# Differential attention scores from full-precision, unsplit queries and keys, a head's two maps as two 64-row products

## The chip, the cores and the metric

The kernel runs on one NeuronCore of a Trainium2 chip. The metric is the device time of one execution in microseconds (us); a lower time is better. Five engines matter here: TensorE (PE in the profile; its weight loads are a row of their own, PEld), VectorE (DVE), ScalarE (ACT), GpSimd (POOL) and SyncE (SP), which issues nearly all DMA transfers. TensorE reads its operands from SBUF, a memory of 128 partitions, and writes to PSUM, which has eight banks of 512 fp32 values in each partition.

## What is computed

The reference is one encoder layer, applied to two groups (prompt and sample) of 1024 tokens with 1024 channels. One projection of the normalised input yields the queries, keys and values of two attention branches and several gates. Branch A is grouped-query attention with 8 heads of 64 dimensions. Branch B is the part that the change touches:

```python
qb = rms_norm(qb.reshape(B, S, H_B, 2, HEAD_DIM), qn_b)      # 4 heads, 2 maps, 64 dims
kb = rms_norm(kb.reshape(B, S, H_B, 2, HEAD_DIM), kn_b)
...                                                           # partial rotary on q and k
s = jnp.einsum('bqhmd,bkhmd->bhmqk', qblk, k) * scale
p = jax.nn.softmax(s, axis=-1)
pd = p[:, :, 0] - lam * p[:, :, 1]
return jnp.einsum('bhqk,bkhe->bqhe', pd, v)                   # 128-dim values
```

Each head of B thus has two score maps of 1024 x 1024. The sum over d in a score has 64 terms. Afterwards both branches are gated, projected, merged and projected once more.

## The kernel before, in words

**Split operands.** Nearly all products run in a TensorE data type (float32r) that takes one pass but keeps fewer bits than fp32. To regain precision, an operand x is split into a high part (a copy rounded to float32r) and a low part (x minus the high part), and the products high-high, high-low and low-high are added in PSUM. `proj_tt` (L497) and `z_gen` (L679) do so with three matmuls for each chunk of the input projection.

**Queries and keys of B.** `qkb_gen` projects the queries and keys of one head, 128 tokens at a time (8 token tiles, `tt`). `rms` and `rope` normalise and rotate them, mostly on POOL. `pairs_T` then transposes them on TensorE (L548) into a PSUM bank, in which partitions 0 to 63 hold map 0 and 64 to 127 hold map 1. For each map it writes one tile that holds the high part in 64 partitions and the low part in the other 64: two ACT copies (L550, 64 x 256) and two DVE subtractions (L551, 64 x 256) for each token tile. A head keeps two such tiles of 128 x 2048 (from `utile`, a pool of 15), one for each map, and each holds queries and keys.

**Scores.** Since high and low parts are stacked in the 128 rows, one matmul gives high-high plus low-low. The crosswise terms need the same queries with the halves exchanged: `swapped` makes that copy with DMAs (L574), two for each map and pair of query tiles. `softmax_unit` computes one map for 128 queries and 1024 keys: for each half of the keys a matmul with the queries (L709) and one with the swapped queries (L710), into a score tile of two PSUM banks (`sbank`; the pool `ps_s` has two of them, so both are in use when two maps are under way). DVE takes the row maximum (L711), and ACT the exponential with its sum (L712), which frees the score tile. `scores` calls this once for each map. After map 1 it also computes the factor lambda x sum0 / sum1 (L731 on DVE, L732 on POOL). `flip` combines the two maps (L744), transposes in blocks (L745), and sends the result through four DMAs (L750). `b_values` multiplies it with the values (L810). The values of B are kept unsplit in fp32 already, so L810 is a full-precision product; the trace shows each as two weight loads and two matmul instructions.

**Order of the work.** `attention` writes the attention as a list of small steps. A unit is 256 queries of one head. In B a unit has four score steps (query tile 0 map 0, map 1, query tile 1 map 0, map 1) and seven value steps that start 1.4 units later. `weave` interleaves these steps with the projections (`qkb_gen`, `vb_gen`, `z_gen`) by shares of progress: `phase` counts `4 * (9 + PV_LAG)`, that is 44, attention steps for a head of B, and the stretch with the last head counts `LAST_ATT`, 48. Attention steps are given a priority 100 instructions ahead of their place (`AHEAD`). A scheduler then fixes the order of the instructions on each engine before the run, by priority among those it takes to be ready. On the chip every engine keeps that order and waits on semaphores.

**Counts.** Two groups, four heads and eight query tiles make 64 query tiles of B, each with two maps. The B score products number 2 x 2 x 128 = 512: 256 on L709 and 256 on L710. Scores of B (L709 writing s from a tile u) start at 512 us for the first group and near 1460 us for the second. Branch A's scores run on the same lines with another operand pair (s from u and u).

Of the kernel before, what the change touches and what calls it, by code (L numbers as in the profile page):

```python
# [12 lines left out]
F32 = mybir.dt.float32  # L13
# [77 lines left out]
def kernel(ctx: ExitStack, tc: tile.TileContext, t: dict):  # L91
# [23 lines left out]
    def sbank():  # L115
        return ps_s.tile([P, 1024], F32, tag="s", name=nm("s"))
# [13 lines left out]
    def utile():  # L130
        return upool.tile([P, 2048], F32R, tag="u", name=nm("u"))
# [448 lines left out]
    def v2(u):  # L580
        return u.rearrange("p (h n) -> p h n", h=2)
# [43 lines left out]

    def qkb_gen(ht, out, h):
        w = load_w(w_cols(w_in, (C_QB + h * P, P), (C_KB + h * P, P)))
        qk = out[h] = (v2(utile()), v2(utile()))

        def front(tt, ps):  # L630
            e = by_turns(tt)
            x3, s3 = rms(ps, 4, e)
            x4 = x3.rearrange("p (a m) d -> p a m d", a=2)
            e.tensor_tensor(out=x4, in0=x4, in1=gB.unsqueeze(2).to_broadcast([P, 2, 2, HD]), op=ALU.mult)
            rope(x3[:, :, :16], s3[:, :, :16], cosB[:, tt], sinB[:, tt], 8, e)
            return x3

        def back(tt, x3):
            sl = slice(tt * P, (tt + 1) * P)
            pairs_T(x3, qk[0][:, :, sl], qk[1][:, :, sl])  # L640
            made[id(qk)] = tt + 1

        yield from pipelined(ht, w, front, back)
# [56 lines left out]
    def piece_order(x):  # L700
        return x.rearrange("p (i t b) -> p i t b", t=2, i=4)

    def softmax_unit(q, sw, k, pt, su):

        m = tiny.tile([P, 1], F32, tag="m", name=nm("m"))
        s = sbank()
        for n in range(2):
            sl = slice(n * 512, (n + 1) * 512)
            nc.tensor.matmul(s[:, sl], q, k[:, sl], start=True, stop=False)  # L709
            nc.tensor.matmul(s[:, sl], sw, k[:, sl], start=False, stop=True)  # L710
        nc.vector.tensor_reduce(out=m, in_=s, axis=AX.X, op=ALU.max, negate=True)  # L711
        nc.scalar.activation(  # L712
            pt.rearrange("p (j c a) -> p j c a", j=4, c=8), s.rearrange("p (c a j) -> p j c a", c=8, j=4),
            AF.Exp, bias=m, accum_out=su,
        )

    def scores(u, i):

        nm_ = len(u["q"])
        t, m = i // nm_, i % nm_  # L720
        qt = u["pr"] * 2 + t
        if "sw" not in u:
            u["sw"] = swapped(u)
        pt = ptile()
        su = u["su"][:, qt : qt + 1] if m == 0 else tiny.tile([P, 1], F32, tag="su", name=nm("su"))
        softmax_unit(u["q"][m][:, qt * P : (qt + 1) * P], u["sw"][:, m, t * P : (t + 1) * P], u["k"][m], pt, su)
        if m == 0:
            u[t] = [pt]
        else:
            f = tiny.tile([P, 1], F32, tag="r", name=nm("r"))  # L730
            nc.vector.reciprocal(f, su)  # L731
            nc.gpsimd.tensor_scalar(  # L732
                out=f, in0=f, scalar1=u["su"][:, qt : qt + 1], scalar2=nlam, op0=ALU.mult, op1=ALU.mult
            )
            u[t] += [pt, f]
        return t if m == nm_ - 1 else None

    def flip(u, t):

# [103 lines left out]
    def attention(units):  # L843


        steps = []
        for n, (ph, _, _) in enumerate(units):
            na, nv = (2, 4 + PV_LAG) if ph < 2 else (4, 5 + PV_LAG)
            steps += [(n + i / na, ph, n, i, True) for i in range(na)]
            steps += [(n + BEHIND + i / nv, ph, n, i, False) for i in range(nv)]  # L850
        steps.sort(key=lambda x: x[0])
        live, vals, late = {}, {}, []
        last = max(x[1] for x in steps)
        cur = 0
        for at, ph, n, i, qk in steps:
            if qk:
                while cur < ph:
                    cur += 1
                    yield cur
            with tc.high_priority(offset=AHEAD):  # L860
                if qk:
                    if n not in live:
                        live[n] = units[n][1]()
                    t = scores(live[n], i)
                else:
                    t = None
                    if n not in vals:
                        vals[n] = (a_values if ph < 2 else b_values)(live[n])
                    next(vals[n], None)
                for todo in late:  # L870
                    todo()
                late = []
                if t is not None:
                    late.append(lambda u=live[n], t=t: flip(u, t))
                    if t == (0 if ph < 2 else 0) and n + 1 < len(units) and units[n + 1][2]():
                        live[n + 1] = units[n + 1][1]()
                        late.append(lambda u=live[n + 1]: u.update(sw=swapped(u)))
            yield None
        for todo in late:
            todo()  # L880
# [135 lines left out]
    def units_of(st):  # L1016

        def a_unit(half, i, pr):
            j = half * 4 + i
            kv = j // 4  # L1020
            return {
                "q": [st["qa"][half][i % 2][:, i // 2]], "k": [st["ka"][:, kv]],
                "v": (lambda k: st["va"][:, k, kv, :]),
                "pr": pr, "j": j, "od": st["od"][j // 2], "su": st["suA"][:, j],
            }

        def b_unit(h, pr):
            qk = st["qkb"][h]
            return {
                "q": [qk[m][:, 0] for m in range(2)], "k": [qk[m][:, 1] for m in range(2)],  # L1030
                "v": st["vb"][h], "pr": pr, "h": h,
                "od": st["od"][4 + h], "ss": st["ssB"], "su": st["suB"][:, h],
            }

        def there(kind, n, pr):
            return made.get(id(st[kind].get(n)), 0) > 2 * pr + 1

        units = []
        for half in range(2):
            units += [  # L1040
                (half, lambda a=(half, i, pr): a_unit(*a), lambda a=("qa", half, pr): there(*a))
                for i in (0, 2, 1, 3) for pr in range(4)
            ]
        for h in range(4):
            units += [
                (2 + h, lambda a=(h, pr): b_unit(*a), lambda a=("qkb", h, pr): there(*a)) for pr in range(4)
            ]
        return units
# [23 lines left out]
    for g in range(2):  # L1072
        st = states[g]
        ht = st["ht"]
        load_tables_A(st)
        zs = chain(*[z_item(st, i) for i in range(12)])
        head(g, st, zs, late)
        alone[0] = False
        if g == 0:
            load_tables_B()  # L1080

        att = attention(units_of(st))

        def phase(k, *fs, more=()):
            n_att = 16 * (6 + PV_LAG) if k < 2 else 4 * (9 + PV_LAG)
            nz = 3 * Z_SHARE[g][k]
            weave(
                (until_next(att), n_att * ATT_W[g][k], 0.0), (chain(*fs), 31 * len(fs), IN_A[g][k]),
                (islice(zs, nz), nz, Z_A[g][k]), *more,
            )  # L1090

        phase(0, qa_gen(st, 1))
        phase(1, vb_gen(ht, st["vb"], 0), qkb_gen(ht, st["qkb"], 0))
        oT, mT = ([], []), ([], [])
        for h in range(4):
            fs = []
            if h < 3:
                fs.append(qkb_gen(ht, st["qkb"], h + 1))
            if h == 1:
                fs.append(vb_gen(ht, st["vb"], 1))  # L1100
            if h < 3:
                phase(2 + h, *fs)

        first = chain(*[gated_gen(st, i, hf, oT[hf]) for i in range(2) for hf in range(2)])
        then = [[gated_gen(st, i, hf, oT[hf]) for hf in range(2)] for i in (2, 3)]

        def gates():
            yield from first
            yield from chain(*then[0])

        def fill():
            if g == 0:
                yield from gate_gen()
            yield from zs
            drain(first)
            yield from islice(merge, 16 - TAIL)

        merge = merge_gen(st, 0, oT, mT)

        weave((until_next(att), LAST_ATT, 0.0), (fill(), LAST_FILL, 0.0), (gates(), 12, GATED_A))  # L1120
        alone[0] = True
        weave((merge, TAIL, 0.0), (then[1][0], 2, TAIL_A))
        weave((merge_gen(st, 1, oT, mT), 8, 0.0), (then[1][1], 4, 1.0))
        if g == 0:
            weave((out_gen(g, mT), 16, 0.0), (ht_gen(1, states[1]["ht"]), 13, -0.1))
        else:
            drain(out_gen(g, mT))
# [54 lines left out]
```

## Time and profile before

| | |
|---|---|
| median of 3 runs | 1982.26 us (1980.13 to 1987.66) |
| span of the profiled execution | 1985.5 us (the profile gives no other time for it) |
| TensorE busy with matmuls / weight loads | 1908.6 us (96%) / 1627.8 us (82%) |
| DVE / ACT / POOL busy | 1330.8 (67%) / 1009.9 (51%) / 758.1 us (38%) |
| mean granted TensorE clock | 0.982 |
| DMA | 295.11 MB |

The span runs from the first to the last instruction of one execution; it stands 3.2 us above the median of the runs. Busy times are unions of the instructions' records. A matmul's record is longer than its share of the array, since consecutive matmuls overlap at their ends, so the cost of a matmul is read from the distance of starts in a long row of equal ones. In the tables of instruction groups a row reads: line, engine, operation, output from inputs, shape, count, then busy time and mean ns of one, then idle time of the engine ahead of it and what ended that.

### The profile page before, as it was taken

The numbers are of one execution on the slowest core, as the hardware profiler recorded it, in microseconds if no ns is written. First come the engines' busy times: TensorE is split into PE (matmuls) and PEld (weight loads), VectorE is DVE, ScalarE is ACT, GpSimd is POOL, SyncE is SP. The second block draws the span as 40 slices with busy tenths as digits, with TensorE's granted clock in tenths as the row PEclk, the third lists the DMA queues.
The fourth block names the chain that finished last, engine by engine and source line by source line (L and its number), as shares of the span: only waits on it lengthen the run. The fifth ranks groups of instructions, "written<-read, shape, count | busy, mean of one in ns | idle before, by whom it ended". The sixth has DMA issues, their size and how long they took to land.

```text
span 1985.5 us, 30670 instructions
## 1 busy us (share of the span) xinstructions
PE 1908.6 (96%) x10466; PEld 1627.8 (82%) x10466; DVE 1330.8 (67%) x1906; ACT 1009.9 (51%) x1939; POOL 758.1 (38%) x1008
## 2 busy tenths in 40 slices
PE   8889999999999998999999899999999999999999
PEld 3878888888878994778888787888887888877887
DVE  4558877777877577547465877677788845665641
ACT  4435655665654444754323565556655534566310
POOL 2374612453446252221235464134445626422110
PEclk9899999999999999999999999999999999999999
DMA  8124556555553345865641455565654333567532
GB/s 310 33 80 126 155 152 169 152 166 154 133 153 102 101 120 173 257 227 167 222 149 35 140 144 145 149 164 144 184 137 137 106 97 99 156 212 245 174 101 75
DMA packets 269531, 295.11 MB, mean 149 GB/s; under 512 B 35776, under 2 KB 218176, under 8 KB 269376
## 3 DMA queue, kind: packets, MB, share of 16 engines
q1 hardware_dynamic: 269376, 293.15, 49.7%
q8 instruction: 84, 1.38, 0.3%
q14 instruction: 71, 0.58, 0.1%
HBM read 133.59 MB, written 42.01 MB: 88 GB/s over the span
## 4 chain that ended last, share of the span: by engine, by line
PE 68%; DMA 8%; DVE 8%; ACT 5%; SPq 4%; issue 3%; POOL 3%; ACTq 0%; POOLq 0%; DVEq 0%
PE f L497 16%; PE f L679 16%; PE f L950 6%; PE f L979 5%; PE s L709 4%; PE a L810 4%; PE s L710 4%; PE s L979 4%; DMA q<-p 3%; SPq L750 3%; PE s L950 2%; DVE q L759 2%; PE a L771 2%; PE a L770 2%; DVE m L711 2%
## 5 line engine op out<-in xcount | busy, mean ns | idle before, releaser
L679 PE MATMUL f<-u,w 128*128 128x512 f32 x2232 | 582.3, 398 | 0.1
L497 PE MATMUL f<-w,u 128*128 128x256 f32 x3456 | 487.0, 286 | 2.2 <-ACT ev L685 1.4
L497 PEld LDWEIGHTS f<-w,u 128*128 128x128 f32 x3456 | 459.5, 192 | 22.4 <-ACT ev L685 1.8
L679 PEld LDWEIGHTS f<-u,w 128*128 128x128 f32 x2232 | 408.8, 190 | 77.3 <-POOL w L181 0.8
L181 POOL TENSOR_TENSOR w<-st,w 128x512 fp32r<-128x512 f32 x168 | 230.3, 1390 | 439.9 <-ACT w L179 375.1
L712 ACT ACTIVATE p<-s,m 128x1024 f32<-128x1024 f32 x256 | 284.4, 1111 | 206.3 <-DVE m L711 111.3
L711 DVE TENSOR_REDUCE m<-s 128x1 f32<-128x1024 f32 x256 | 310.0, 1216 | 51.3 <-PE s L710 48.7
L745 DVE STREAM_TRANSPOSE p<-p 128x1024 f32<-128x1024 f32 x192 | 238.2, 1241 | 99.2 <-ACT p L712 86.5
L759 DVE TENSOR_TENSOR q<-q,hi 128x512 fp32r<-128x512 f32 x256 | 198.3, 792 | 60.6 <-ACT hi L758 58.6
L515 POOL TENSOR_TENSOR rs<-ss,nhalf 128x4 f32<-128x4 f32 (+1 forms) x112 | 112.8, 1007 | 322.8 <-DVE ss L514 284.0
L758 ACT ACTIVATE hi<-q 128x512 fp32r<-128x512 f32 x256 | 153.8, 625 | 104.1 <-DMA q<-p 55.4
L710 PE MATMUL s<-u,sw 128*128 128x512 f32 x512 | 206.7, 404 | 0.0
L179 ACT ACTIVATE w<-st 128x512 fp32r<-128x512 f32 x196 | 113.9, 625 | 97.2 <-DMA st<-in_w_in_dram 46.0
L950 PE MATMUL f<-u,w 128*128 128x512 f32 x552 | 133.4, 395 | 5.1 <-ACT ev L685 4.4
L770 PE MATMUL a<-hi,u 128*128 128x256 f32 x512 | 132.5, 285 | 2.1 <-DVE oo L787 2.1
L771 PE MATMUL a<-q,u 128*128 128x256 f32 x512 | 129.8, 286 | 1.2 <-DVE q L759 1.2
L810 PE MATMUL a<-q,u 128*128 128x256 f32 x512 | 128.3, 390 | 1.9 <-DVE oo L826 1.5
L950 PEld LDWEIGHTS f<-u,w 128*128 128x128 f32 x552 | 103.9, 190 | 27.2 <-ACT ev L685 4.7
L709 PE MATMUL s<-u 128*128 128x512 f32 x256 | 110.9, 433 | 15.1 <-ACT p L712 15.1
L810 PEld LDWEIGHTS a<-q,u 128*128 128x128 f32 x512 | 97.8, 196 | 17.5 <-DVE oo L826 1.6
L709 PE MATMUL s<-u,u 128*128 128x512 f32 x256 | 103.6, 405 | 8.3 <-ACT p L712 7.7
L710 PEld LDWEIGHTS s<-u,sw 128*128 128x128 f32 x512 | 98.4, 192 | 15.5
(175 smaller groups left out, 2562.1 us busy)
## 6 DMA issues: line engine op xcount, KB each, us to landing
q<-p SPq DMA_DIRECT2D x768, 128.0 KB, 2.6
st<-in_w_in_dram SPq DMA_DIRECT2D x132, 256.0 KB, 3.0
zd<-ev SPq DMA_DIRECT2D x96, 256.0 KB, 2.2
sw<-u SPq DMA_DIRECT2D x256, 64.0 KB, 2.1
p<-zd SPq DMA_DIRECT2D x64, 256.0 KB, 3.2
u<-in_w_ada_dram SPq DMA_DIRECT2D x8, 1024.0 KB, 10.4
st<-in_w_in_dram SPq DMA_DIRECT2D x64, 128.0 KB, 2.7
st<-in_w_out_dram SPq DMA_DIRECT2D x32, 256.0 KB, 2.9
```

The costliest lines, as they stand in the source:

```text
L181: e.tensor_tensor(out=wl, in0=st, in1=wh.bitcast(F32), op=ALU.subtract)
L497: nc.tensor.matmul(ps, lt[c][:, sl], w[:, c, wi, :], start=(k == 0), stop=(k == 23))
L679: nc.tensor.matmul(ps, w[:, c, wi, e * P : (e + 1) * P], rt[c], start=(k == 0), stop=(k == 23),)
L709: nc.tensor.matmul(s[:, sl], q, k[:, sl], start=True, stop=False)
L710: nc.tensor.matmul(s[:, sl], sw, k[:, sl], start=False, stop=True)
L711: nc.vector.tensor_reduce(out=m, in_=s, axis=AX.X, op=ALU.max, negate=True)
L712: nc.scalar.activation(pt.rearrange("p (j c a) -> p j c a", j=4, c=8), s.rearrange("p (c a j) -> p j c a", c=8, j=4), AF.Exp, bias=m, accu ...
L745: nc.vector.transpose(pt, pt)
L759: nc.vector.tensor_tensor(out=tl, in0=tl.bitcast(F32), in1=th.bitcast(F32), op=ALU.subtract)
L810: nc.tensor.matmul(acc, u["v"][:, k], pT[:, k], start=(k == 0), stop=(k == 7))
L950: nc.tensor.matmul(ps, w[:, c, wi, d * P : (d + 1) * P], o[:, oi, :], start=(k == 0), stop=(k == 11))
L979: nc.tensor.matmul(ps, w[:, c, wi, e * P : (e + 1) * P], m[:, mi, :], start=(k == 0), stop=(k == 23))
```

## The change

The queries and keys of B are no longer split. Each head has one fp32 tile of 128 x 2048: map 0 in partitions 0 to 63, map 1 in 64 to 127, queries in the first half of the columns and keys in the second. `qkb_gen` fills it with one ACT copy of 128 x 256 for each token tile. `scores_b` computes both maps of a query tile in one step: for each half of the keys one fp32 product for map 0 (64 rows, into the first score tile) and one for map 1 (the other 64 rows, into the second). Maximum, exponential and factor follow as before. The swapped copies are not made for B. A unit of B has two score steps in place of four, and `phase` counts 36 steps for a head; `LAST_ATT` stays 48. Branch A does what it did.

```diff
     def qkb_gen(ht, out, h):
         w = load_w(w_cols(w_in, (C_QB + h * P, P), (C_KB + h * P, P)))
-        qk = out[h] = (v2(utile()), v2(utile()))
+        qk = out[h] = v2(utile().bitcast(F32))
...
         def back(tt, x3):
-            sl = slice(tt * P, (tt + 1) * P)
-            pairs_T(x3, qk[0][:, :, sl], qk[1][:, :, sl])
+            ps = gbank()[:, : 2 * P].rearrange("p (b n) -> p b n", b=2)
+            x = x3.rearrange("p (b two) d -> p b (two d)", two=2)
+            for b in range(2):
+                nc.tensor.transpose(ps[:, b, :], x[:, b, :], ident)
+            nc.scalar.activation(qk[:, :, tt * P : (tt + 1) * P], ps, AF.Copy)
             made[id(qk)] = tt + 1
...
+    def scores_b(u, t):
+        qt = u["pr"] * 2 + t
+        ss = [sbank(), sbank()]
+        for n in range(2):
+            sl = slice(n * 512, (n + 1) * 512)
+            for s, rows in zip(ss, (LO, HI)):
+                nc.tensor.matmul(
+                    s[:, sl], u["qk"][rows, 0, qt * P : (qt + 1) * P], u["qk"][rows, 1, sl], start=True, stop=True
+                )
+        pts = [ptile(), ptile()]
+        sus = [u["su"][:, qt : qt + 1], tiny.tile([P, 1], F32, tag="su", name=nm("su"))]
+        for s, pt, su in zip(ss, pts, sus):
+            softmax(s, pt, su)
+        f = tiny.tile([P, 1], F32, tag="r", name=nm("r"))
+        nc.vector.reciprocal(f, sus[1])
+        nc.gpsimd.tensor_scalar(out=f, in0=f, scalar1=sus[0], scalar2=nlam, op0=ALU.mult, op1=ALU.mult)
+        u[t] = [*pts, f]
+        return t
...
-            na, nv = (2, 4 + PV_LAG) if ph < 2 else (4, 5 + PV_LAG)
+            na, nv = (2, 4 + PV_LAG) if ph < 2 else (2, 5 + PV_LAG)
...
-                        late.append(lambda u=live[n + 1]: u.update(sw=swapped(u)))
+                        if ph < 2 and "q" in live[n + 1]:
+                            late.append(lambda u=live[n + 1]: u.update(sw=swapped(u)))
...
-            n_att = 16 * (6 + PV_LAG) if k < 2 else 4 * (9 + PV_LAG)
+            n_att = 16 * (6 + PV_LAG) if k < 2 else 4 * (7 + PV_LAG)
```

`softmax` is the second half of `softmax_unit` (maximum and exponential), taken out as a function; `LO` and `HI` are the partition slices 0 to 63 and 64 to 127.

More of the change, by code (lines that the diff above doesn't have):

```diff
@@ L701, in piece_order, with softmax @@
         return x.rearrange("p (i t b) -> p i t b", t=2, i=4)
+    def softmax(s, pt, su):
+        m = tiny.tile([P, 1], F32, tag="m", name=nm("m"))
+        nc.vector.tensor_reduce(out=m, in_=s, axis=AX.X, op=ALU.max, negate=True)
+        nc.scalar.activation(
+            pt.rearrange("p (j c a) -> p j c a", j=4, c=8), s.rearrange("p (c a j) -> p j c a", c=8, j=4),
+            AF.Exp, bias=m, accum_out=su,
+        )
     def softmax_unit(q, sw, k, pt, su):
-        m = tiny.tile([P, 1], F32, tag="m", name=nm("m"))
         s = sbank()
@@ L710, in softmax_unit @@
             nc.tensor.matmul(s[:, sl], sw, k[:, sl], start=False, stop=True)
[L711 to L715, printed above, removed]
+        softmax(s, pt, su)
[7 more added lines that the diff above has]
+                    s[:, sl], u["qk"][rows, 0, qt * P : (qt + 1) * P], u["qk"][rows, 1, sl], start=True, stop=True
+                )
+        pts = [ptile(), ptile()]
+        sus = [u["su"][:, qt : qt + 1], tiny.tile([P, 1], F32, tag="su", name=nm("su"))]
+        for s, pt, su in zip(ss, pts, sus):
+            softmax(s, pt, su)
+        f = tiny.tile([P, 1], F32, tag="r", name=nm("r"))
[3 more added lines that the diff above has]
+        return t
     def scores(u, i):
-        nm_ = len(u["q"])
-        t, m = i // nm_, i % nm_
+        if "qk" in u:
+            return scores_b(u, i)
+        t = i
         qt = u["pr"] * 2 + t
@@ L724, in scores @@
         pt = ptile()
[L725 to L736, printed above, removed]
+        su = u["su"][:, qt : qt + 1]
+        softmax_unit(u["q"][0][:, qt * P : (qt + 1) * P], u["sw"][:, 0, t * P : (t + 1) * P], u["k"][0], pt, su)
+        u[t] = [pt]
+        return t
     def flip(u, t):
@@ L1027, in b_unit @@
         def b_unit(h, pr):
-            qk = st["qkb"][h]
             return {
-                "q": [qk[m][:, 0] for m in range(2)], "k": [qk[m][:, 1] for m in range(2)],
-                "v": st["vb"][h], "pr": pr, "h": h,
+                "qk": st["qkb"][h], "v": st["vb"][h], "pr": pr, "h": h,
                 "od": st["od"][4 + h], "ss": st["ssB"], "su": st["suB"][:, h],
```

## The prediction

> **What bounds the kernel now.** I read the first and the fourth part of the page, then a table of the two stretches in which branch B's attention runs.
>
> ```profile
> span 1985.5 us, 30670 instructions
> PE 1908.6 (96%) x10466; PEld 1627.8 (82%) x10466; DVE 1330.8 (67%) x1906; ACT 1009.9 (51%) x1939; POOL 758.1 (38%) x1008
> PE 68%; DMA 8%; DVE 8%; ACT 5%; SPq 4%; issue 3%; POOL 3%; ACTq 0%; POOLq 0%; DVEq 0%
> ```
>
> TensorE is busy for 96% of the span and holds 68% of the chain that ended last; no other engine exceeds 67% or 8%.
>
> ```profile
> 512.00:860.00 348.00, 329.42 (x1771) 273.29 (x1770) 237.97 (x333) 188.07 (x345) 142.08 (x222) 0.98 0.53 156
> 1470.00:1830.00 360.00, 340.81 (x1854) 294.66 (x1853) 243.17 (x343) 198.84 (x362) 155.63 (x226) 0.98 0.51 150
> ```
>
> The columns are length, then busy time and count of PE, PEld, DVE, ACT and POOL, the granted clock, and DMA. In B's stretches TensorE is idle for 18.6 and 19.2 us, 37.8 us together. DVE is busy for 68% of them. So work taken from DVE, ACT or the DMA queue can give back at most those 37.8 us there, while a microsecond of TensorE time added costs nearly a microsecond. The question is what the score products cost on TensorE.
>
> **Removed from TensorE.** The rows of the B products, by shape, and one query tile's eight products in the order of time:
>
> ```profile
> L709 PE MATMUL s<-u 128*128 128x512 f32 x256 | 110.9, 433 | 15.1 <-ACT p L712 15.1
> L710 PE MATMUL s<-u,sw 128*128 128x512 f32 x512 | 206.7, 404 | 0.0
> ```
>
> ```profile
> 709.94 0.39 PE L709 MATMUL s<-u 128*128 128x512 f32 x1
> 710.17 0.39 PE L710 MATMUL s<-u,sw 128*128 128x512 f32 x1
> ...
> 711.53 0.40 PE L710 MATMUL s<-u,sw 128*128 128x512 f32 x1
> 711.77 0.39 PE L548 MATMUL f<-ident,row 128*128 128x128 f32 x2
> ```
>
> Each record lasts 0.39 us, but they start 0.23 us apart: eight take 711.77 - 709.94 = 1.83 us. L709 has 256 such products for B and half of L710's 512 are B's, so 64 query tiles go at 1.83 us: **-117 us**.
>
> **Added to TensorE.** The kernel already has one full-precision product, L810. The chain of waits, in order of time, has a run of it beside runs of the one-pass products:
>
> ```profile
> 586.44 3.45 PE a L810 x16
> 593.56 2.87 PE f L497 x24
> 597.36 1.82 PE f L679 x8
> ```
>
> An instruction of L810 (256 columns) takes 3.45 / 16 = 0.216 us, one of L497 (256 columns, one pass) 0.120 and one of L679 (512 columns, one pass) 0.228. L810 has 512 instructions for 256 products of the program, two for each. Doubling the columns multiplies the one-pass price by 1.9, so an instruction of a full-precision product with 512 columns costs between 1.9 x 0.216 = 0.41 and 2 x 0.216 = 0.43 us; I take 0.43. A query tile gets four products (two maps, two halves of the keys), eight instructions of 0.43 us. That only 64 of the 128 rows are used does not shorten a stream of 512 columns.
>
> What matters is how many of the eight lie on top of each other, and no row of before shows a 64-row product. Three cases:
> - *None overlap:* 8 x 0.43 = 3.44 us, 220 us for 64 tiles, +103 us net.
> - *All overlap in pairs:* 4 x 0.43 = 1.72 us, 110 us, -7 us net.
> - *Chained:* TensorE takes its matmuls in program order. A product's second instruction needs the rows that its first one occupies, so map 1's first instruction starts beside map 0's second: first; second with other first; and so on. That is five slots for eight instructions, 2.15 us, 138 us, **+21 us** net.
>
> The row nearest in kind, L810, gives the price of one instruction, which I use. Whether two of them overlap it cannot say. I choose the chained case, since the two maps read disjoint halves of the partitions and write different PSUM banks, so that nothing in the operands ties them, and in-order issue alone keeps them from full pairing.
>
> The Trainium skill (TensorE: Matmul & The Clock Gate, "Part 3: Packing small matmuls — row/col tiling") says that products in different row groups run concurrently while matmuls start and end in program order. By it the sum would have the chained term. The Trainium skill (TensorEngine Tiling (Array Packing), "Theoretical Speedup") puts two tiles at up to twice the rate, which would be the paired term. No row here shows either.
>
> **Broken bursts.** The scheduler sometimes puts other products between the scores:
>
> ```profile
> 603.98 0.40 PE L709 MATMUL s<-u 128*128 128x512 f32 x1
> 604.21 0.28 PE L497 MATMUL f<-w,u 128*128 128x256 f32 x1
> 604.33 0.40 PE L710 MATMUL s<-u,sw 128*128 128x512 f32 x1
> 604.57 0.28 PE L497 MATMUL f<-w,u 128*128 128x256 f32 x1
> ```
>
> A full-height product in between ends an overlap. Today that costs nothing; then it would cost up to 3.44 - 2.15 = 1.29 us a tile. The bounds are 0 and 64 x 1.29 = 83 us. I estimate that a quarter of the tiles lose half of it: 16 x 0.65 = **+10 us**.
>
> **Changing between full height and half height.** No row shows it. The nearest are the weight load, and how far a matmul's record outlasts its stream:
>
> ```profile
> L709 PEld LDWEIGHTS s<-u 128*128 128x128 f32 x256 | 49.0, 192 | 33.3 <-ACT p L712 20.1 <-issue 3.1 <-ACT row L905 0.9
> L810 PE MATMUL a<-q,u x512: 377/379/634, 555.9 to 1811.9; 128*128 128x256 f32 x171
> ```
>
> At best a change is free. At worst the array empties (0.379 - 0.216 = 0.16 us) and the next weight load (0.19 us) no longer hides behind a stream: 0.35 us. Two changes for each of 64 tiles give 0 to 45 us. I take the emptying alone, 128 x 0.16 = **+21 us**. The weight loads themselves stay at eight for each tile and hide as L810's do.
>
> The Trainium skill (TensorEngine Tiling (Array Packing), "Key Properties") speaks against the change here: a change of tiling mode drains TensorE. By it the 21 us are due, without it the term is 0; no row here shows which.
>
> **The other engines.** Rows of the first B stretch, then the page's row of the swapped copies:
>
> ```profile
> L551 DVE TENSOR_TENSOR u<-f,u 64x256 fp32r<-64x256 f32 x44 | 18.5, 422 | 11.5 <-ACT u L550 10.3
> L550 ACT ACTIVATE u<-f 64x256 fp32r<-64x256 f32 x44 | 16.5, 374 | 14.2 <-DVE u L551 6.9 <-PE f L548 6.7
> L509 ACT ACTIVATE row<-f 128x256 f32<-128x256 f32 x20 | 7.6, 381 | 22.9 <-PE f L497 17.0 <-POOL row L517 2.0 <-POOL row L634 2.0
> ```
>
> ```profile
> sw<-u SPq DMA_DIRECT2D x256, 64.0 KB, 2.1
> ```
>
> For 64 token tiles (two groups, four heads, eight each) two subtractions of 0.422 us go: DVE -54 us. Two ACT copies of 0.374 become one of 128 x 256, priced like L509's 0.381: ACT -23 us. Half of the 256 copy transfers go, with their places on SP's queue. All of this lies beside TensorE's work. It gains only where TensorE waits:
>
> ```profile
> PE s L709 <- ACT p L712: 7.1, 3, 4.0
> PE f L548 <- POOL row L537: 5.1, 2, 3.9
> PE s L709 <- ACT p L712: 8.0, 8, 1.9
> ```
>
> The scores wait 15.1 us in all for a score tile (the first row is of the first stretch, the third of the second) and transposes 5.1 us for POOL, which the change does not relieve. The bounds are 0 and the 37.8 us of idle time; I take **-12 us**. The freed tile of 128 x 2048 for each head, and the eight fewer steps for a head against an unchanged `LAST_ATT`, are costed at nothing beyond that bound: TensorE's own queue covers both.
>
> **The new wait.** A query tile now needs both score tiles at once. The rows:
>
> ```profile
> L711 DVE TENSOR_REDUCE m<-s 128x1 f32<-128x1024 f32 x256 | 310.0, 1216 | 51.3 <-PE s L710 48.7
> L712 ACT ACTIVATE p<-s,m 128x1024 f32<-128x1024 f32 x256 | 284.4, 1111 | 206.3 <-DVE m L711 111.3 <-DMA q<-p 84.4 <-DVE r L731 3.0
> ```
>
> Two maxima of 1.22 us and the last exponential of 1.11 us free the second tile 3.5 us after the products end. Query tiles come every 348 / 32 = 10.9 us, so the cover is ample on average. Where it is gone, every projection behind the scores in TensorE's queue waits too, and their readers after them.
>
> **The sum:** 21 + 10 + 21 - 12 = +40 us on the profiled execution's 1985.5 us, 2025.5 us. That execution lies 3.2 us above the median of the runs (1982.26), so the forecast is **2022 us**.
>
> **Rivals.**
> 1. *The two maps do not run side by side; the change does not do what it says.* +103 us, changes of height +21, and more idle time and the last heads' DMA waits get filled (-25): +99, 2081 us; 2060 to 2125 by the bounds (no changes of height; all of them and nothing filled). For it: every row of before shows one stream at a time at its full price, and two instructions for each product make pairing harder. Against it: the operands are disjoint.
> 2. *Faster.* The maps pair fully (1.72 in place of 1.83 us) at no cost for the changes of height, and the scores' 15.1 us of waiting go, since score tiles return sooner with DVE 54 us lighter: -7 - 15 = -22, 1960 us. It decides from the point where a tile takes less than about 2.0 us on TensorE, all included. Against it: program order, and the broken bursts.
> 3. *Score tiles become the wait.* Both maps' products are queued together, and TensorE stands up to 3.5 us at a tile that comes too early. If one tile in four does, 16 x 3.5 = 56 us, 2078 us; its sign would be idle time ahead of the score products far above 15.1 us.
>
> **How the numbers follow.** Forecast (chained, 1995 to 2055): 0.5. Rival 1: 0.3. Rival 2: 0.1. Rival 3: 0.05. The remaining 0.05 is chained with cheap changes of height, near 1982. About 0.5% (10 us) is what a measurement of this kernel can tell from no change: faster 0.1, within it 0.08, slower 0.82. The range reaches down to 1985, leaving out rival 2 and part of the cheap case, and up to 2100, leaving out the upper fifth of rival 1.
>
> **What would show it.** Chained: the records of a tile's eight score instructions overlap in time, map 1's first starting within some ns of map 0's second, and the tile spans about 2.2 us. Rival 1: starts every 0.43 us, a span of 3.4. Changes of height: a gap of 0.16 us or more between a 128-row product and the first 64-row one. The two fp32 copies L550 and L551 of B are gone, DVE's busy time is down by about 54 us. I am wrong if the 64-row price per instruction is not 0.43 us, or if TensorE's idle time in B's stretches moves by more than 38 us.

## The result, and the profile after

The changed kernel takes 2064.99 us (median of 3 runs, 2059.72 to 2066.97) against 1982.26 us before: a recorded ratio of 1.0400, with a 95% interval of 1.0368 to 1.0432 (the two medians alone give 1.042). It is 83 us slower; the forecast was 40 us slower.

The page of the changed kernel, the span, the busy times and the chain that ended last:

```profile
span 2063.1 us, 30289 instructions
PE 2010.6 (97%) x10466; PEld 1594.5 (77%) x10466; DVE 1270.7 (62%) x1778; ACT 983.3 (48%) x1874; POOL 750.9 (36%) x1008
...
PE 81%; DMA 4%; issue 4%; DVE 4%; ACT 3%; POOL 2%; SPq 2%; ACTq 0%; POOLq 0%; DVEq 0%
```

The span grew by 77.6 us (the profiled execution before stood 3.2 us above the median of its runs, this one 1.9 us below). TensorE's busy time grew by 2010.6 - 1908.6 = 102.0 us, and the rest of the span shrank from 1985.5 - 1908.6 = 76.9 to 52.5 us, by 24.4. So the loss is TensorE time, and a quarter of it is made up by smaller gaps. TensorE's share of the chain rose from 68% to 81%; those of DVE and of the DMA transfers fell from 8% to 4% each and that of ACT from 5% to 3%. DVE is 60 us lighter and ACT 27 us, and that bought at most these gaps.

The score products by shape, then the two stretches in which B's attention now runs:

```profile
L730 PE MATMUL s<-u 64*128 64x512 f32 x512 | 225.5, 626 | 6.3 <-ACT p L710 6.3
```

```profile
512.00:900.00 388.00, 380.21 (x1768) 260.11 (x1767) 217.77 (x288) 176.90 (x318) 142.24 (x220) 0.98 0.46 133
1510.00:1900.00 390.00, 384.84 (x1788) 270.64 (x1788) 214.97 (x280) 180.89 (x324) 143.97 (x224) 0.99 0.42 124
```

There are 512 instructions of 64 x 512, as forecast. Their union is 225.5 us, far from the 138 of the chained case. (A union can't be set beside these sums directly, since it also holds the longer first start and last record of every unbroken row: below, four streams of 0.43 us, 1.72 in all, have a union of 1.98. The places are counted below.) TensorE stands idle for 7.8 and 5.2 us in these stretches (18.6 and 19.2 before).

The order of time shows why. Two moments of the changed kernel, first one with the two maps apart, then one with them together:

```profile
589.73 2.32 PE L497 MATMUL f<-w,u 128*128 128x256 f32 x18
591.99 1.98 PE L730 MATMUL s<-u 64*128 64x512 f32 x4
593.90 1.58 PE L497 MATMUL f<-w,u 128*128 128x256 f32 x11
```

```profile
613.02 0.38 PE L642 MATMUL f<-ident,row 128*128 128x128 f32 x2
613.33 1.99 PE L730 MATMUL s<-u 64*128 64x512 f32 x8
615.25 2.58 PE L682 MATMUL f<-u,w 128*128 128x512 f32 x10
```

Four instructions alone take 1.98 us, and so do eight when both maps stand together. Inside the eight, records start two by two, 6 or 7 ns apart, and the pairs 0.43 us apart (0.53 from the first to the second). **The two halves of the array do run side by side, and fully. The kernel mostly does not let them.** Call a piece an unbroken row of B's score instructions on TensorE, and a place the 0.43 us that one instruction, or a pair side by side, takes. In the trace the 512 instructions stand in 131 pieces; 68 hold one map's four instructions and 38 a single product, and only 13 hold eight instructions in four pairs (some of these join a tile's map 1 to the next tile's map 0). In all 74 of 256 possible pairs formed, which leaves 512 - 74 = 438 places.

The order of TensorE's instructions, fixed before the run, shows the same 131 pieces. Here is the first query tile: both halves of the keys of map 0 (tile s_965), seventeen rows of other work, then map 1 (s_966):

```
2170 L730 MATMUL s_965_5607<-u_660_3850 128x512 x2
2171 L497 MATMUL f_964_5597<-w_928_5361,u_110_553 128x256
...
2187 L682 MATMUL f_973_5625<-u_77_327,w_945_5473 128x512
2188 L730 MATMUL s_966_5608<-u_660_3850 128x512 x2
```

Map 0's score tile comes free one exponential ahead of map 1's, so map 0's products are ready first and go first.

### The profile page after: what moved, and what is told of

It is laid out like the page before. It is cut to its first block, busy times and chain, and to the rows that moved or that the text cites. A ratio compares the mean times of both kernels' runs of the same rounds, so it can differ in the third digit from the quotient of the medians.

```text
span 2063.1 us, 30289 instructions
## 1 busy us (share of the span) xinstructions
PE 2010.6 (97%) x10466; PEld 1594.5 (77%) x10466; DVE 1270.7 (62%) x1778; ACT 983.3 (48%) x1874; POOL 750.9 (36%) x1008
## 4 chain that ended last, share of the span: by engine, by line
PE 81%; DMA 4%; issue 4%; DVE 4%; ACT 3%; POOL 2%; SPq 2%; ACTq 0%; POOLq 0%; DVEq 0%
PE f L682 20%; PE f L497 18%; PE s L730 8%; PE f L970 5%; PE f L999 5%; PE a L829 4%; PE s L999 3%; PE s L720 3%; PE a L789 3%; PE a L790 3%; PE s L721 2%; PE s L970 2%; SPq L769 1%; DMA q<-p 1%; DMA row<-zd 1%
## 5 line engine op out<-in xcount | busy, mean ns | idle before, releaser
L497 PEld LDWEIGHTS f<-w,u 128*128 128x128 f32 x3456 | 452.3, 190 | 54.5 <-issue 30.3
L497 PE MATMUL f<-w,u 128*128 128x256 f32 x3456 | 486.8, 286 | 2.2 <-ACT ev L688 1.4
L730 PE MATMUL s<-u 64*128 64x512 f32 x512 | 225.5, 626 | 6.3 <-ACT p L710 6.3
L730 PEld LDWEIGHTS s<-u 64*128 64x128 f32 x512 | 72.4, 186 | 84.8 <-issue 63.1
L739 POOL TENSOR_SCALAR r<-r,suB,nlam 128x1 f32<-128x1 f32 x64 | 22.5, 351 | 263.9 <-DVE r L738 263.6
```

What stands on the lines that cost most here:

```text
L497: nc.tensor.matmul(ps, lt[c][:, sl], w[:, c, wi, :], start=(k == 0), stop=(k == 23))
L730: nc.tensor.matmul(s[:, sl], u["qk"][rows, 0, qt * P : (qt + 1) * P], u["qk"][rows, 1, sl], start=True, stop=True)
```

## The experiments

Three theories of why it is slower than forecast. **Order:** pairs overlap where they stand together, the fixed order keeps most apart, and each piece pays for a change to half height and back. **Price:** full-precision 64-row products are dear wherever they stand. **Wait:** needing both score tiles at once is what costs. The price of going to half height for one piece and back (one excursion) was read ahead of the runs from the rows at 589.73 to 593.90 above. An L497 record lasts 0.28 us, and the next one starts 0.12 us behind it. The last L497 of the first row starts at 589.73 + 2.32 - 0.28 = 591.77, so the next instruction would start at 591.89; the eleven behind the piece end at 595.48, so the last of them starts at 595.20 and the first in effect at 594.00. Of the 2.11 us between, four instructions of 0.43 us are 1.72; 0.39 us remains, half of it going in and half coming out by the records. Six more pieces of the trace with one map's four instructions between rows of L497 give the same, 0.386 to 0.395 us.

**One score tile for both maps.**

```diff
-    ps_s = ent(tc.tile_pool(name="ps_s", bufs=2, space=PSUM))
+    ps_s = ent(tc.tile_pool(name="ps_s", bufs=1, space=PSUM))
...
+    s_both = ps_s.tile([P, 2048], F32, tag="s", name="s_both")
+    s_turn = [0]
     def sbank():
-        return ps_s.tile([P, 1024], F32, tag="s", name=nm("s"))
+        s_turn[0] ^= 1
+        return s_both[:, 1024:] if s_turn[0] else s_both[:, :1024]
```

> The changed kernel with one PSUM tile of four banks for both maps in place of two tiles that come free one after the other, so that the order fixed before the run keeps a query tile's four products together: in 58 of 64 query tiles they stand in one piece, against 13 in the changed kernel. Order theory (the pairs overlap where they stand together, and the changed kernel loses them because the second map's tile comes free later): the score instructions take about 270 places of 0.43 us in place of 438, and some 75 entries and exits of 0.39 us in place of 131, so 145 us of TensorE in place of 239; with TensorE's idle time back at what it was before the change, 1985 us, and 1965 to 2010. Price theory (full-precision 64-row products cost what they cost, wherever they stand): 2065, within 10. Wait theory (needing both score tiles at once is what costs): over 2065, with idle time ahead of the score products well over 15 us.

The same edit on the kernel before:

> Control: the kernel before, unchanged but for the one PSUM tile of four banks in place of two tiles. If that tile by itself makes nothing faster or slower, 1982 us within 10 (order theory). If it moves the kernel by more, the gain of the run with the one tile on the changed kernel must be read against this one.

Measured: 2247.72 us on the changed kernel (ratio 1.1317, 1.1289 to 1.1346), 2277.16 on the kernel before (1.1471, 1.1448 to 1.1494). No theory had that. The control tells what happened. Its rows of B's score products, then of A's (operands u and u), by what ended the idle time ahead of them:

```profile
L713 PE MATMUL s_both<-u 128*128 128x512 f32 x256 | 121.7, 475 | 96.8 <-ACT p L716 94.1 <-DMA q<-p 2.6
L713 PE MATMUL s_both<-u,u 128*128 128x512 f32 x256 | 112.6, 440 | 32.4 <-ACT p L716 32.4
```

With one tile the scores wait 126.5 us for exponentials, 94.1 of it in branch B and 32.4 in branch A; in the kernel before, with two tiles, both together wait 22.8. The halves no longer alternate: none of the 512 products on this line starts while a maximum or an exponential of scores is running, where 143 of 512 do in the kernel before. The granted clock (the mean share of its full speed that TensorE was allowed) fell too, to 0.920 from 0.982, and the same 10466 matmuls are busy for 2021.9 us in place of 1908.6. Of the 294 us by which the span grew, 113 are thus slower matmuls and 181 time in which TensorE is not busy. On the changed kernel the clock is 0.931. So the edit tests nothing about B by its total. Beside its own control the changed kernel is 29 us ahead instead of 83 behind, and its score instructions have a union of 148.6 us in place of 225.5, which speaks for the order theory, but not cleanly. A third run with the one tile, on split operands in pairs (the form shown further down), was forecast at 1945 to 1985 us by the order theory and 2060 by the price theory. It took 2213.07 us (1.1145, 1.1122 to 1.1168), at a clock of 0.935, and tells as little.

**Full height by padding.** The queries of each map are padded with zeros.

```diff
...
-                nc.tensor.matmul(s[:, sl], u["qk"][rows, 0, qt * P : (qt + 1) * P], u["qk"][rows, 1, sl], ...)
+                nc.tensor.matmul(s[:, sl], qp[:, m, qt * P : (qt + 1) * P], kk[:, sl], ...)
```

> The changed kernel with the queries of each map padded with zeros to 128 rows, so that every product is of full height: nothing can overlap, and TensorE never changes between full and half height. ACT makes three copies for each token tile in place of one. Order theory with 0.39 us for each entry and exit: 512 x 0.43 = 220 us of TensorE for the scores, against 188 + 51 = 239 in the changed kernel, so about 2045 us, 2030 to 2060. If changing height costs nothing, the 74 pairs lost cost 32 us: 2097, over 2080.

Measured: 2063.82 us (1.0399, 1.0379 to 1.0418), between the two numbers, so the time decides nothing. The page does better:

```profile
PE 1995.5 (97%) x10466; PEld 1617.9 (79%) x10466; DVE 1274.1 (62%) x1778; ACT 1008.8 (49%) x2004; POOL 762.8 (37%) x1024
```

TensorE is busy 15.1 us less than in the changed kernel (19 forecast with the price for height, 32 more without it), and the span of 2059.2 us holds 11 us more that is not busy. All the overlap of the changed kernel was worth less than its changes of height.

**Both score tiles freed together.** Branch A is untouched. The score products also go ahead of other ready work.

```diff
+        with tc.high_priority(offset=1000):
             for n in range(2):
...
+        held = tiny.tile([P, 1], F32, tag="held", name=nm("held"))
+        nc.vector.scalar_tensor_tensor(
+            out=held, in0=ss[0][:, :1], scalar=sus[1], in1=sus[1], op0=ALU.mult, op1=ALU.add
+        )
         nc.vector.reciprocal(f, sus[1])
```

> The changed kernel, branch A untouched. One small DVE operation reads a column of map 0's score tile and the sum of map 1's exponential, so that map 0's tile comes free only when map 1's does, and the score products go ahead of other work that is ready. In the fixed order 57 of 64 query tiles then have their four products in one piece, in 71 pieces in all (changed kernel: 13 and 131). Order theory: about 272 places of 0.43 us and 71 entries and exits of 0.39 us, 145 us of TensorE in place of 239: 94 us less, of which the return of idle time takes 20 to 40, so 1995 us, 1980 to 2020. Price theory: 2065 within 10. Wait theory: over 2065, with much idle time ahead of the score products, since map 0's tile is held a microsecond longer.

The priority without the joint release:

> The changed kernel with the score products ahead of other ready work, but without the joint release. In the fixed order the two maps of a query tile then stand apart almost always (114 of 127 pieces hold one map's two products alone, 24 of 256 pairs can overlap). Order theory: 488 places of 0.43 us and 127 entries and exits of 0.39 us, 260 us against 239 in the changed kernel, so 2080 us, 2068 to 2100. If the priority by itself is what helps in the other run, this one falls below 2050.

Measured: 2044.14 us with the joint release (1.0318, 1.0275 to 1.0361) and 2107.77 without it (1.0629, 1.0589 to 1.0670). Both missed their ranges on the slow side, but the order of the two is as the order theory has it, and they differ in one DVE operation only. Their score rows, freed together first:

```profile
L731 PE MATMUL s<-u 64*128 64x512 f32 x512 | 143.8, 629 | 18.7 <-ACT p L710 18.6
```

```profile
L731 PE MATMUL s<-u 64*128 64x512 f32 x512 | 247.5, 621 | 5.2 <-ACT p L710 5.2
```

The same 512 instructions have a union of 143.8 us in 71 pieces or of 247.5 in 127. **The price theory falls:** nothing about a product changed but what stands next to it. The page of the kernel with the joint release tells what took the gain back; under it the main waits:

```profile
span 2039.9 us, 30398 instructions
PE 1937.7 (95%) x10466; PEld 1582.7 (78%) x10466; DVE 1270.7 (62%) x1842; ACT 983.5 (48%) x1878; POOL 747.0 (37%) x1008
```

```profile
PE s L731 <- ACT p L710: 18.6, 9, 3.9
PE f L642 <- POOL row L537: 11.0, 4, 5.2
...
PE a L834 <- DMA q<-p: 8.6, 3, 4.7
```

TensorE is busy 72.9 us less than in the changed kernel (94 forecast), but the time it is not busy doubles, from 52.5 to 102.2 us. The scores wait 18.6 us for score tiles (6.3 in the changed kernel), the transposes 11.0 us for POOL, the value products 8.6 us for their transposed scores. So a part of the wait theory holds once TensorE is relieved. The granted clock is another part: it is 0.980 in place of 0.988 over the span, and 0.96 in B's stretches in place of 0.98 and 0.99. By that ratio some 16 of the 1937.7 busy us are slower matmuls (an estimate), and at equal clock TensorE would be relieved by about 89 us, close to the 94 forecast. The run without the joint release fits as well: its TensorE is busy for 2044.9 us, 34.3 more than in the changed kernel, of which by the clock of 0.982 some 12 are slower matmuls; 21 were forecast. What lowers the clock these runs don't isolate.

**Is POOL what is late?** Every second token tile's rotation goes to DVE.

```diff
-            e = by_turns(tt)
+            e = nc.vector if tt % 2 == 0 else nc.gpsimd
```

> As the run with the joint release, with the rotation of every second token tile of B's queries and keys on DVE in place of POOL. If the idle time that took back half of that run's gain comes from POOL being late with the transposes' input (11 us of waiting for it there), 2030 us, 2020 to 2036. If it comes from elsewhere, or DVE becomes late with the score maxima, 2044 or more.

Measured: 2046.26 us (1.0325, 1.0281 to 1.0370), as without it. The transposes' wait for POOL fell from 11.0 to 2.8 us, but one of 5.4 us for DVE came in, and the time that TensorE is not busy stayed, 102.5 us after 102.2. Relieving POOL in this way gives nothing.

**Split operands in pairs**, with the priority and the joint release, which has the least TensorE time of the paired forms (1918.2 us busy):

```diff
...
-                nc.tensor.matmul(s[:, sl], u["qk"][rows, 0, ...], u["qk"][rows, 1, sl], start=True, stop=True)
+            for j, (a, b) in enumerate(((0, 0), (0, 1), (1, 0))):
+                for s, rows in zip(ss, (LO, HI)):
+                    nc.tensor.matmul(s[:, sl], u["qk"][a][rows, 0, qs], u["qk"][b][rows, 1, sl], start=(j == 0), stop=(j == 2))
...
```

> As the run with the joint release, but with queries and keys split into a high and a low tile and three one-pass 64-row products (high-high, high-low, low-high; the low-low term is left out) in place of each full-precision one. Order theory: six paired places of 0.23 us and one entry and exit of 0.39 us for each query tile, some 116 us, as much as the 117 us of the kernel before, with the swapped copies and half of the ACT and DVE splitting gone: 1975 us, 1955 to 1995. Price theory: 12 places of 0.23 us a tile, 2060.

> As the run with split operands in pairs and the joint release (the low-low term is left out), with the rotation of every second token tile of B's queries and keys on DVE in place of POOL. If POOL is what holds the transposes, 1995 us, 1985 to 2003; if not, 2007 or more. Only below 1982 would it beat the kernel before.

Measured: 2007.24 us (1.0126, 1.0091 to 1.0160), and 2023.22 (1.0195, 1.0157 to 1.0234) with the rotations shared out. The first misses its range on the slow side by 12 us, and sharing out the rotations costs 16 us more where a gain was hoped for. The first is 37 us better than full-precision pairs, where 20 were forecast, and still 22 us behind the kernel before. Nothing here beats that kernel.

**Both maps in one step, nothing else.**

```diff
     def scores(u, i):
+        if len(u["q"]) > 1:
+            score(u, 2 * i)
+            return score(u, 2 * i + 1)
+        return score(u, i)
...
```

> Control: the kernel before, with its split operands and its eight one-pass products, but with both maps of a query tile in one attention step (two score steps for a unit, 36 steps counted for a head), as in the changed kernel. If the grouping of the steps by itself costs or gains nothing: 1982 us within 12. If it is what costs, 2000 or more.

Measured: 1998.12 us (1.0068, 1.0042 to 1.0093): 13 us over the kernel before as measured beside it, and so between the two numbers, nearer to 2000. In its profile of 1993.5 us TensorE's busy time is what it was (1909.6 us; 1908.6 before), and the rest of the span is 83.9 us in place of 76.9. The grouping costs about ten microseconds of waiting, a small wait of the third theory's kind. The changed kernel has the same grouping.

**The change of height by itself.** The kernel before gets one more short product ahead of each map's scores, of half height and, as a control, of full height.

```diff
+            if n == 0 and b:
+                nc.tensor.matmul(s[:, :256], q[LO], k[LO, :256], start=True, stop=True)
             nc.tensor.matmul(s[:, sl], q, k[:, sl], start=True, stop=False)
```

> The kernel before with one more product ahead of each map's scores of branch B: one pass, 64 rows, 256 columns, into columns that the score products overwrite. It adds 128 streams of 0.12 us and 128 changes to half height and back. If one such excursion costs 0.39 us beside its stream, as read from the changed kernel, it adds 15 + 50 us: 2045 us, 2030 to 2065, and stands some 45 us above the run with the same products at full height. If the price in the changed kernel belongs to full-precision products and not to the height, both runs are alike, near 2000.

> Control for the run with half height: the same added product with all 128 rows. 128 streams of 0.12 us, 15 us on TensorE: 2000 us, 1988 to 2012 in both theories.

Measured: 2033.98 us (1.0251, 1.0222 to 1.0280) and 2007.09 (1.0118, 1.0093 to 1.0143). The order of time, half height and then full height:

```profile
605.51 1.46 PE L497 MATMUL f<-w,u 128*128 128x256 f32 x11
606.91 0.38 PE L710 MATMUL s<-u 64*128 64x256 f32 x1
607.22 0.50 PE L711 MATMUL s<-u 128*128 128x512 f32 x1
607.55 0.39 PE L712 MATMUL s<-u,sw 128*128 128x512 f32 x1
```

```profile
615.44 3.22 PE L497 MATMUL f<-w,u 128*128 128x256 f32 x24
618.50 0.28 PE L710 MATMUL s<-u 128*128 128x256 f32 x1
618.62 0.40 PE L711 MATMUL s<-u 128*128 128x512 f32 x1
618.86 0.40 PE L712 MATMUL s<-u,sw 128*128 128x512 f32 x1
```

From the added product to the second score product it takes 0.64 us at half height and 0.36 at full; on the way in another 0.1 us is lost (the last L497 starts at about 606.69, 0.22 ahead in place of 0.12). That is 0.38 us for one excursion, with one-pass products: **the price belongs to the height**, not to full precision. It is no single case: over 34 added products of each run that follow a row of L497, the median way from the last L497 to the second score product is 0.853 us at half height and 0.473 at full, again 0.38 apart. Of 128 x 0.38 = 49 us the pages show 38.5 as busy time (1959.3 against 1920.8 us), and the spans differ by 24.0 us (2029.7 against 2005.7), so 14.5 us went into gaps. The half-height run had the higher granted clock, 0.988 against 0.983; by that ratio its busy time would have been some 10 us longer at equal clock (an estimate), which makes up the 49.

## Why the prediction came out as it did

It was right in direction, in the bound (TensorE's own time) and in the range. The range held in part by luck: 2065 us lies outside the 1995 to 2055 of the forecast's own case and inside rival 1's, and the stated range took in most of both. Of its 40 us, step by step:

- **Removed (-117) and the price of an instruction (0.43 us): right.** The pairs start 0.43 us apart.
- **"Chained", +21: the wrong mechanism.** It rested on TensorE taking matmuls in program order, so that map 1 would start beside map 0's second instruction. In the trace map 1's first record starts 6 ns after map 0's first, though map 0's second stands ahead of it in the order. (A record does not name its map; by the order of the products, two that run at once can only be one of each.) Where the order has both products of one map ahead of the other's, the pairs form as well (13 or 14 ns apart). A whole piece takes four places, not five. The Trainium skill (TensorE: Matmul & The Clock Gate, "Part 3: Packing small matmuls — row/col tiling") has concurrency and strict program order; the first agrees with this trace (6 or 7 ns between the starts of a pair), the second does not hold for products of different row groups here.
- **"Broken bursts", +10: the step that failed.** I guessed that a quarter of the tiles would lose half their overlap, from the kernel before, where a break cost nothing. The records show 512 - 74 = 438 places of 0.43 us, 188 us, which is +71 in place of the -7 of full pairing: 78 us lost to the order. I had written under the new wait that the second score tile comes free last, and costed it as waiting only. It decides the order too, as a scheduler that goes by readiness issues map 0 alone: holding map 0's tile until map 1's was free took the pieces from 127 to 71 and the union from 247.5 to 143.8 us.
- **Height, +21: too small for the same reason.** I priced a change at 0.16 us and took two for each of 64 tiles. It is 0.195, twice for each of 131 pieces: +51. The rule of the Trainium skill that spoke against the change (TensorEngine Tiling (Array Packing), "Key Properties": changing the mode drains TensorE) agrees with the two added-product runs in that an excursion has a price, 0.38 us there. Whether TensorE empties in it, these runs do not show.
- **Idle time, -12: -24.4**, of which the wait for score tiles gave 8.8 (15.1 to 6.3 us). In B's stretches alone it fell from 37.8 to 13.0 us, inside the bounds of 0 and -37.8.

By these, 71 + 51 - 24 = +98 against 77.6 measured. The busy time accounts for 102 of the 122; of the other 20 some 12 are the granted clock (0.988 in place of 0.982 over 2010 us), and 8 stay unexplained.

Rival 1 (2081 us; its upper bound adds up to 2130 and not 2125) came nearer in time than the forecast, for half the right reason: most maps do not run side by side, but because of where they stand, not because they cannot. Rival 2's full pairing was true of the hardware, and its other condition, no cost for height, was not. Rival 3 is not what the changed kernel suffers from (6.3 us of waiting for score tiles against 15.1), though it appears as soon as TensorE is relieved.

What stays open: why the time that is not busy doubles when the pairs form. Of the 50 us, the priority by itself brings 11 (63.4 us not busy in the run without the joint release) and the joint release the other 39; of these the scores' wait for their tiles is some 13. The grouping of steps can't explain it, since the changed kernel has it too, and relieving POOL did not help. Why the granted clock fell when the pairs formed is open as well. Whether shares of progress fitted to the new lengths would recover the rest wasn't tried.

## What to carry to other kernels

Operations that gain by standing next to each other need inputs and output buffers that become free at the same moment; otherwise a scheduler that goes by readiness takes them apart, and the gain is gone while the costs stay. Price the excursion, not the instruction: count the pieces that the order will make, each with its way in and out. And when the bounding engine is relieved by some microseconds in a kernel that is 96% busy, expect a good part of them back as waiting, here 50 of 73. Read the granted clock beside the busy time: a difference of 0.008 over the span is worth some 16 us here, as much as some of the effects that were looked for.

## What the runs showed of the hardware that was not expected

- Two 64-row products in different halves of the array run fully side by side, in either program order, when no 128-row product stands between them: eight instructions in 1.99 us, as four alone take 1.98.
- One excursion from full height to half and back costs 0.38 to 0.39 us of TensorE time beside its streams, for one-pass products (read at 34 of them) and full-precision ones (read at 7 pieces) alike.
- A PSUM tile whose halves are used in turn does not replace two tiles: in the kernel before it cost 292 us, some 181 as time not busy and 113 as the same matmuls at a granted clock of 0.920 in place of 0.982 (by the spans, 294 in all).
